# Eight dense column blocks of the first expert table, later choices for the second row block, earlier dot products and two rings of query weights

## The chip, the cores and the metric

The kernel runs on one core of a Trainium2 chip. The time is the device time of one execution in microseconds (us): lower is better. Five engines take part, each with its own queue of instructions: TensorE (PE, with its weight loads listed apart as PEld), VectorE (DVE), ScalarE (ACT), GpSimd (POOL) and SyncE (SP). SP issues most plain DMA transfers, POOL the gathers of single rows by index.

## The reference

One decoder layer on 256 prompt tokens and 32 sample tokens: a joint input projection, RWKV-7 heads and sparse-attention heads, an output projection, a layer norm, an expert mixer (PEER) and a second layer norm. The change concerns the first half of the expert mixer. Cut to it:

```python
def peer_ffn(x, wq, subkeys, u_tab, v_tab):            # x: 256 x 2048; 8 heads, 128 keys
    q = (xt @ wq).reshape(n, P_HEADS, 2, P_DKEY // 2)
    s = einsum('nhcd,hckd->nhck', q, subkeys)
    hv, hix = top_k(s, 16)
    cand   = hv[:, :, 0, :, None] + hv[:, :, 1, None, :]
    cand_e = hix[:, :, 0, :, None] * 128 + hix[:, :, 1, None, :]
    tv, tpos = top_k(cand, 16)
    expert = take_along_axis(cand_e, tpos)              # 8 x 16 experts of 16384 per token
    gate = softmax(tv)
    h = gelu(einsum('cd,chkd->chk', xb, u_tab[expert])) # 128 dot products per token
    return einsum('chk,chkd->cd', gate * h, v_tab[expert])
```

The tables `u_tab` and `v_tab` have 16,384 rows of 2,048 numbers each.

## The kernel before

The 256 prompt tokens are two row blocks of 128 (`t` = 0 and 1), a token to a partition. A dot product of a token with one of its chosen rows of the first table is split by columns:

- The first `UG` = 128 x (16 - `NDB`) = 896 columns are gathered. For each of the 2 x 128 pairs of row block and choice, POOL issues one indirect DMA (L454, `rows<-in_peer_u_g,gi`: 128 rows of 896 numbers into one of `NRW` = 5 buffers named `rows`, called by `fetch`), and DVE multiplies them with the tokens (`x1a`) and sums up in one instruction (`dot`, L1794). The indices lie in `gi`. There are 256 such dots.
- The other `NDB` = 9 blocks of 128 columns are computed densely for all 16,384 rows: for each of 128 steps `i1`, SP loads 128 x 1152 numbers of the transposed table (L1864, `ur<-in_peer_u_t`, `NUR` = 5 buffers), PE does nine matmuls against the transposed tokens `Xfd` (L1867), and ACT copies the 128 x 256 sums to `AW` (L1868). The numbers that were chosen are picked from `AW` later, in the weigh stage, and added to the dots.

Ahead of this dense loop stands the query loop over nine steps `h`. In step `h` SP loads the query weights of head `h` (`query_load`, L1711, 512 KB each, a ring of `WB` = 4 buffers `wraw`), PE projects them, and ACT copies the queries to `QP`. The scores of head `h - 1` follow (`scores`, both row blocks, into a ring of four `TB`), and then its choices (`choose`, both row blocks): on DVE three times the top 16 with their indices (L1363 to L1367), the sums over 54 candidates (L1400), and a comparison of each chosen position with an iota (L1409, 128 x 864, into a `rows` buffer `hit`); POOL multiplies `hit` with the candidates' expert numbers (L1411). One step later `settle` sums `hit` up on DVE (L1417) and copies the 16 expert numbers to `gi` on POOL (L1418). DVE also does four dots of the sample tokens (`sr`, L1556) per step. From `h` = 7 one prompt dot per step is put in (`NDW` = 1).

After the query loop stand the softmax of both row blocks (`gates`), and the dense loop with two dots per step `i1` until 256 are done (`dot`). `table(0)` writes the first row block's indices, gates and sums transposed into `TB` within the loop; `table(1)` comes in the weigh stage. That stage reuses the `rows` buffers for its sample rows (`smp_fetch`), and the loads of the second table (`rows_load`, L1971, `v_`) begin in it. Its first load stands on SP's queue wherever the scheduler puts it.

What order the instructions have on each queue is set by a scheduler, which takes the program's order and its own estimates; `issue_after(x)` makes it place what stands inside behind instruction `x`. Buffers come from named pools with a number of copies (`bufs`); a new use waits until the old one is read.

Of the kernel before, what the change touches and what calls it, by code (L numbers as in the profile page):

```python
# [18 lines left out]
P = 128  # L19
# [3 lines left out]
NPR = 256  # L23
# [126 lines left out]
def hybrid_decode_step(ctx: ExitStack, tc: tile.TileContext, a, outs, dbg=None):  # L150
# [1218 lines left out]
    def scores(t, h, pool, QP, SKT, tag):  # L1369


        pb = bank(tag)
        for c in range(2):
            if t < 2:
                pe.matmul(pb[:, 128 * c:128 * c + 128], QP[:, 2 * h + c, P * t:P * t + P], SKT[:, 2 * h + c, :],
                          start=True, stop=True)
            else:
                for g in range(4):
                    k = 2 * (2 * g + h) + c
                    pe.matmul(pb[32 * g:32 * g + 32, 128 * c:128 * c + 128], QP[:, k, :], SKT[:, k, :],  # L1380
                              start=True, stop=True)
        S = TB[:, (2 * h + t) % 4].rearrange("p (a b) -> p a b", a=2) if t < 2 else pool([P, 2, P], "S")
        sc.copy(S.rearrange("p a b -> p (a b)"), pb[:, :256])
        return S

    def choose(t, h, pool, S, TV):

        nb_ = 2 if t < 2 else 1
        HV, HI, HF = (pool([P, 2, 16], nm, ty, bufs=nb_) for nm, ty in (("HV", F32), ("HI", U32), ("HF", F32)))
        for c in range(2):  # L1390
            top16(S[:, c, :], HV[:, c, :], HI[:, c, :])
        k_ = 2.0 if t == 2 else 1.0
        for c in range(2):
            gp.tensor_scalar(HF[:, c], HI[:, c], k_ if c else k_ * P, 0.0, op0=OP.mult, op1=OP.add)

        CV, CE = (pool([P, NCAND], nm, bufs=nb_) for nm in ("CV", "CE"))
        for dst, src, en in ((CV, HV, ve), (CE, HF, gp)):
            o = 0
            for i0, ni, w in CAND:
                en.tensor_tensor(dst[:, o:o + ni * w].rearrange("p (i j) -> p i j", i=ni),  # L1400
                                 src[:, 0, i0:i0 + ni, None].to_broadcast([P, ni, w]),
                                 src[:, 1, None, :w].to_broadcast([P, ni, w]), OP.add)
                o += ni * w
        TI, TF = (pool([P, 16], nm, ty, bufs=nb_) for nm, ty in (("TI", U32), ("TF", F32)))
        hit = up([P, 1024], "rows", bufs=NRW) if t < 2 else pool([P, 1024], "cw", bufs=NCW)
# [3 lines left out]
        i_ = ve.tensor_tensor(hit, iota[:, None, :NCAND].to_broadcast([P, 16, NCAND]),  # L1409
                              TF[:, :, None].to_broadcast([P, 16, NCAND]), OP.is_equal)  # L1410
        gp.tensor_tensor(hit, hit, CE[:, None, :].to_broadcast([P, 16, NCAND]), OP.mult)  # L1411
# [295 lines left out]
    wring = lambda: kw_([P, 8, P], "wraw", bufs=WB)  # L1707
    def query_load(c, o):

        w = wring()  # L1710
        sy.dma_start(w, w_q[:, 128 * c:128 * c + 128].rearrange("(k p) c -> p k c", p=P)[:, o:o + 8])  # L1711
        return w

    wq_ = {(0, o): query_load(0, o) for o in (0, 8)}

    M_("ln1")
# [50 lines left out]
    up([P, 1024], "rows", bufs=NRW)  # L1767
# [3 lines left out]
    dp, kc, kq = (Pool(nm, "left") for nm in ("dp", "kc", "kq"))  # L1771
    dp([P, NDB, P], "ur", bufs=NUR)
    Xfd = dp([P, NDB, NPR], "Xfd")
    SKT = kq([P, 16, P], "SKT")
    QP = kq([P, 16, NPR], "QP")

    dots = [(t, s_) for t in range(2) for s_ in range(P)]
    got, rows_ = [0, 0], {}

    def fetch(upto):  # L1780

        for i in range(got[0], min(upto, len(dots))):
            t, s_ = dots[i]
            rows_[i] = up([P, 1024], "rows", bufs=NRW)[:, :UG]
            gather(rows_[i], a["peer_u_g"], GI[t][:, s_:s_ + 1])
            got[0] = i + 1

    def dot(n=1, upto=2 * P, keep=False, ahead=NRW):

        for i in range(got[1], min(got[1] + n, upto)):  # L1790
            t, s_ = dots[i]
            fetch(min(i + ahead, upto))
            r_, h_ = rows_.pop(i), HD[t][:, s_:s_ + 1]
            i_ = ve.scalar_tensor_tensor(r_, r_, 1.0, X1a[t], op0=OP.mult, op1=OP.mult, accum_out=h_)  # L1794
# [18 lines left out]
    sy.dma_start(SKT, a["subkeys_t"])  # L1813
    hits = []
    for h in range(9):
        S = []
        for c in (2 * h, 2 * h + 1):
            if c < 16:
                pb = bank("pj")
                for o in range(0, 16, 8):  # L1820
                    w = wq_.pop((c, o), None) or query_load(c, o)
                    for k in range(8):
                        pe.matmul(pb[:, :NPR], w[:, k, :], XT[:, o + k, :], start=(o + k == 0), stop=(o + k == 15))
                last_ = sc.copy(QP[:, c, :], pb[:, :NPR])
            if h and c == 2 * h:
                S = [scores(t, h - 1, kc, QP, SKT, "pb") for t in range(2)]
        if h == 2:
            for t in range(2):
                sy.dma_start(X1a[t], X1D[P * t:P * t + P, :UG])
        if h:  # L1830
            late_, hits = hits, []
            for t in range(2):
                chosen, hit = choose(t, h - 1, kc, S[t], TV[t])
                hits.append(hit)
            with tc.issue_after(chosen.ins):
                for t, hit in enumerate(late_):
# [22 lines left out]
    AW = aw([P, 2, NPR, 64], "AW")

    def dense(i1):

        w = dp([P, NDB, P], "ur", bufs=NUR)
        sy.dma_start(w.rearrange("p k e -> p (k e)"), a["peer_u_t"][P * i1:P * i1 + P, :])  # L1864
        ph = bank("ph")
        for e in range(NDB):
            mm = pe.matmul(ph[:, :NPR], w[:, e, :], Xfd[:, e, :], start=(e == 0), stop=(e == NDB - 1))  # L1867
# [74 lines left out]

    x4p([P, 4, P], "oT", bufs=2)
    ws = x4p([P, 32, 32], "ws")
    fs, sr = bank("fs"), {}

    def smp_fetch(j):

        for q in range(2):
            sr[j, q] = up([P, 1024], "rows", bufs=NRW)  # L1950
            gather(sr[j, q], vh2, ig[q][:, j:j + 1])

    def smp_add(j):
# [16 lines left out]
        raw[k] = (vp if k % 3 else vr)([P, FD], "v_", bufs=2 if k % 3 else 1)  # L1970
        return sy.dma_start(raw[k], vtab[P * k:P * k + P, :FD])  # L1971

    dot(2 * P - got[1])
# [178 lines left out]
```

## Time and profile before

| what | us |
|---|---|
| median of 3 runs (lowest, highest) | 2457.12 (2453.75, 2460.82) |
| the profiled execution | 2451.44 |
| its span, first to last instruction | 2449.7 |
| PE busy | 2254.7 (92%) |
| DVE busy | 1748.2 (71%) |
| POOL busy | 1332.6 (54%) |
| ACT busy | 819.9 (33%) |
| all DMA: 684.09 MB | mean 279 GB/s |
| mean granted TensorE clock | 0.950 |

The span lies 1.7 us under the time of the execution. The busy times are totals over stages of different kinds: the input projection and the heads up to about 1040 us, the query loop from about 1050 to 1220, the dense loop from about 1185 to 1696, then the weigh stage and the product with the second table. The change touches the query and the dense loop, so these stretches are read apart.

### The profile page before, as it was taken

Reading aid. Unit: us, or ns where it says so; the run is one execution under the profiler, and the core shown is the slowest. Engines: PE = TensorE matmul, PEld = TensorE weight load, DVE = VectorE, ACT = ScalarE, POOL = GpSimd, SP = SyncE. Lnnn points to the kernel's source line nnn. Section 1 sums busy time; section 2 is a strip of 40 time slices with the busy share of each in tenths; the row PEclk is TensorE's granted clock in tenths of the full one; section 3 lists DMA queues with packets and bytes.
Section 4 is the critical chain, followed back from the end, with each engine's and each line's share of the span. In section 5 each row is a group of like instructions: output and inputs, shape, how many; then the busy total and the mean of one; then the engine's idle time right before and its main releaser. Section 6 shows DMA issues by size and latency. Waiting matters only on the chain.

```text
span 2449.7 us, 42718 instructions
## 1 busy us (share of the span) xinstructions
PE 2254.7 (92%) x15628; PEld 1886.4 (77%) x15628; DVE 1748.2 (71%) x3985; ACT 819.9 (33%) x1591; POOL 1332.6 (54%) x1419
## 2 busy tenths in 40 slices
PE   7989999997988997779989999998998999999996
PEld 7977898884645665568878888887777888887885
DVE  5789766555653456789955555556777799998888
ACT  4433223223431333220111111111777544444343
POOL 5678423233445003567757555666442688876762
PEclk9999999998996996999999999999999999999998
DMA  7887975448668984988499999998664799999994
GB/s 221 233 247 224 281 213 167 136 141 261 213 228 250 312 277 160 320 287 271 147 402 399 400 403 388 390 400 313 190 190 131 280 359 365 357 369 361 353 346 187
DMA packets 327602, 684.09 MB, mean 279 GB/s; under 512 B 82270, under 2 KB 200992, under 8 KB 326464
## 3 DMA queue, kind: packets, MB, share of 16 engines
q1 hardware_dynamic: 246176, 342.58, 42.1%
q0 software_dynamic: 81216, 338.78, 38.4%
q8 instruction: 123, 2.02, 0.3%
q14 instruction: 87, 0.71, 0.1%
HBM read 665.69 MB, written 23.88 MB: 281 GB/s over the span
## 4 chain that ended last, share of the span: by engine, by line
PE 51%; issue 13%; DVE 12%; POOL 11%; DMA 9%; ACT 2%; SPq 1%; POOLq 0%; DVEq 0%; ACTq 0%
PE pb L2066 20%; POOL rows L454 9%; PE pj L423 8%; PE pa L1660 3%; PE px L1904 3%; PE pa L1937 2%; DVE sr L1556 2%; PE p L1080 2%; PE pt L1896 2%; DMA co<-in_cache_cmp_kv,gidx 2%; PE ss L1497 1%; DMA rows<-in_peer_u_g,gi 1%; PE fs L1955 1%; DVE CA L477 1%; DMA co<-in_cache_sel_kv,sidx 1%
## 5 line engine op out<-in xcount | busy, mean ns | idle before, releaser
L1867 PE MATMUL ph<-Xfd,ur 128*128 128x256 f32 x2304 | 500.8, 380 | 10.1 <-DMA ur<-in_peer_u_t 9.7
L1867 PEld LDWEIGHTS ph<-Xfd,ur 128*128 128x128 f32 x2304 | 439.2, 191 | 71.0 <-issue 10.0
L454 POOL DMA_INDIRECT rq<-in_peer_v_g,gi x256 | 377.6, 1475 | 153.2 <-DVE fP L2039 88.4
L1794 DVE SCALAR_TENSOR_TENSOR rows<-rows,x1a 128x896 f32<-128x896 f32 x256 | 282.0, 1103 | 197.0 <-DMA rows<-in_peer_u_g,gi 195.9
L454 POOL DMA_INDIRECT rows<-in_peer_u_g,gi x256 | 293.1, 1145 | 184.8 <-DVE rows L1794 152.8
L423 PE MATMUL pj<-XH,wl 128*128 128x288 f32 (+1 forms) x752 | 232.2, 309 | 11.3 <-DVE wl L418 6.4
L423 PE MATMUL pj<-XH,wh 128*128 128x288 f32 (+1 forms) x752 | 230.4, 306 | 13.0 <-DVE ss L753 5.9
L2039 DVE SCALAR_TENSOR_TENSOR fP<-rq,ge,fP 128x640 f32<-128x640 f32 x254 | 223.7, 881 | 7.8 <-DMA rq<-in_peer_v_g,gi 5.5
L423 PE MATMUL pj<-XL,wh 128*128 128x288 f32 (+1 forms) x752 | 226.6, 301 | 0.0
L1868 ACT COPY AW<-ph 128x256 f32<-128x256 f32 x128 | 77.0, 609 | 405.9 <-PE ph L1867 400.2
L2066 PE MATMUL pb<-vl,ah 128*128 128x512 f32 (+1 forms) x768 | 207.0, 378 | 0.8
L2066 PE MATMUL pb<-vh,al 128*128 128x512 f32 (+1 forms) x768 | 205.3, 375 | 0.0
L2066 PE MATMUL pb<-vh,ah 128*128 128x512 f32 (+1 forms) x768 | 186.7, 378 | 13.4 <-ACT vh L2058 10.9
L416 ACT CAST wh<-wraw 128x512 fp32r<-128x512 f32 (+1 forms) x188 | 114.6, 616 | 224.1 <-PE pj L423 178.5
L2066 PEld LDWEIGHTS pb<-vh,ah 128*128 128x128 f32 x768 | 144.8, 195 | 35.7 <-ACT vh L2058 13.9
L477 DVE SCALAR_TENSOR_TENSOR CA<-co,wbc,CA 128x256 f32<-128x256 f32 x248 | 135.9, 586 | 49.7 <-DMA co<-in_cache_cmp_kv,gidx 49.7
L2066 PEld LDWEIGHTS pb<-vl,ah 128*128 128x128 f32 x768 | 144.9, 195 | 23.0 <-DVE vl L2059 3.8
L423 PEld LDWEIGHTS pj<-XH,wl 128*128 128x128 f32 (+1 forms) x752 | 144.4, 192 | 22.4 <-DVE wl L418 9.1
L2066 PEld LDWEIGHTS pb<-vh,al 128*128 128x128 f32 x768 | 145.0, 194 | 19.4
L423 PEld LDWEIGHTS pj<-XH,wh 128*128 128x128 f32 (+1 forms) x752 | 144.9, 193 | 19.4 <-DVE ss L753 6.4
L423 PEld LDWEIGHTS pj<-XL,wh 128*128 128x128 f32 (+1 forms) x752 | 144.9, 193 | 1.5 <-issue 1.2
L418 DVE TENSOR_TENSOR wl<-wraw,wh 128x512 fp32r<-128x512 f32 (+1 forms) x141 | 100.2, 720 | 40.0 <-ACT wh L416 39.8
(844 smaller groups left out, 4331.4 us busy)
## 6 DMA issues: line engine op xcount, KB each, us to landing
ur<-in_peer_u_t SPq DMA_DIRECT2D x128, 576.0 KB
wraw<-in_w_in SPq DMA_DIRECT2D x152, 256.0 KB
cw<-in_w_out SPq DMA_DIRECT2D x32, 512.0 KB
wraw<-in_w_out SPq DMA_DIRECT2D x32, 512.0 KB
wraw<-in_peer_wq SPq DMA_DIRECT2D x32, 512.0 KB
cw<-in_peer_wq SPq DMA_DIRECT2D x32, 512.0 KB
wraw<-in_w_in SPq DMA_DIRECT2D x64, 128.0 KB
co<-in_state_win_kv SPq DMA_DIRECT2D x16, 512.0 KB
```

Source lines behind the costliest of these rows:

```text
L416: sc.copy(wh[:, :, :n], w[:, :, :n])
L418: i_ = en.tensor_tensor(wl[:, :, :n], w[:, :, :n], wh[:, :, :n].bitcast(F32), OP.subtract)
L423: last[2] = pe.matmul(pb[:n, :nt], wi[:, k, :n], xi[(o + k) // 8][:, (o + k) % 8, :nt], start=(o + k == 0 and wi is wh and xi is xh), stop ...
L454: gp.indirect_dma_start(out=dst, out_offset=None, in_=rows_, in_offset=bass.IndirectOffsetOnAxis(ap=ix, axis=0))
L477: ve.scalar_tensor_tensor(d_, x_, w_, d_, op0=OP.mult, op1=OP.add)
L1660: pe.matmul(acc[t], xi[:, e, P * t:P * t + P], wi[:, e, :], start=(k == e == n_ == 0), stop=(k == 6 and e == 1 and n_ == 2))
L1794: i_ = ve.scalar_tensor_tensor(r_, r_, 1.0, X1a[t], op0=OP.mult, op1=OP.mult, accum_out=h_)
L1867: mm = pe.matmul(ph[:, :NPR], w[:, e, :], Xfd[:, e, :], start=(e == 0), stop=(e == NDB - 1))
L1868: return mm, sc.copy(AW[:, i1 // 64, :, i1 % 64], ph[:, :NPR])
L1904: pin(pe.matmul(px[:, 128 * e:128 * e + 128].rearrange("p (c j) -> p c j", c=2), oT[:, e, :], AW[:, :, 4 * u + e, :], start=True, stop=True))
L2039: ve.scalar_tensor_tensor(fP[t], r_, w_, fP[t], op0=OP.mult, op1=OP.add)
L2066: pe.matmul(acc[3 * t + q][:, :n_], wi[:, P * t:P * t + P], xi[:, 512 * q:512 * q + n_], start=(k == 0 and wi is ah and xi is vh), stop=(k ...
```

## The change

- `NDB` goes from 9 to 8: a block load has 1,024 columns, PE does eight matmuls per step, and a gathered row has 1,024 numbers (`UG` = 1024).
- The query loop does the choices of the first row block only. The second row block's scores are kept in `S1`; its choices are done in the dense loop by a new generator, `choose_parts`, whose six parts per head are spread, with the dots, over the first 80 steps (`NCB` = 10 steps per head). There DVE does all of it, ACT copies the expert numbers, and it has buffers of its own but for `hit`, which is one of the five `rows`. `gates(1)` follows at step 80, `table(0)` at step 90.
- From `h` = 3 on, `NDW` = 5 dots are put into each query step: 30 in all. The other 226 are spread evenly over the 128 dense steps.
- Query weights go through two rings: the first half of each column group through a second ring `wraw2` of 4 buffers, the other half through `wraw`. `QP` becomes a ring of six.
- The two loads of `x1a` are placed behind the 13th and behind the last query weight, and all loads of `ur` behind the last query weight.
- The `rows` buffers get a pool of their own that ends with the dense loop; the weigh stage takes other ones.

```diff
-NDW = 1
-ND = 1
-NDN = 8
+NDW = 5
+NCB = 10
-NDB = 9
+NDB = 8
...
-        S = TB[:, (2 * h + t) % 4].rearrange("p (a b) -> p a b", a=2) if t < 2 else pool([P, 2, P], "S")
+        S = (TB[:, h % 4], S1[:, h])[t].rearrange("p (a b) -> p a b", a=2) if t < 2 else pool([P, 2, P], "S")
...
+    def choose_parts(h, pool, S, TV):
+        HV, HI, HF = (pool([P, 2, 16], nm, ty) for nm, ty in (("HVb", F32), ("HIb", U32), ("HFb", F32)))
+        for c in range(2):
+            top16(S[:, c, :], HV[:, c, :], HI[:, c, :])
+            yield 1
...
+        TI, TF = (pool([P, 16], nm, ty) for nm, ty in (("TIb", U32), ("TFb", F32)))
+        top16(CV, TV[:, h, :], TI)
+        ve.tensor_copy(TF, TI)
+        yield 1
+        hit = rp([P, UG], "rows", bufs=NRW)[:, :16 * NCAND].rearrange("p (a b) -> p a b", a=16)
+        ve.tensor_tensor(hit, iota[:, None, :NCAND].to_broadcast([P, 16, NCAND]),
+                         TF[:, :, None].to_broadcast([P, 16, NCAND]), OP.is_equal)
+        ve.tensor_tensor(hit, hit, CE[:, None, :].to_broadcast([P, 16, NCAND]), OP.mult)
+        yield 1
+        EF = pool([P, 16], "EFb")
+        ve.tensor_reduce(EF, hit, AX.X, OP.add)
+        sc.copy(GI[1][:, 16 * h:16 * h + 16], EF)
+        yield 1
...
-        w = wring()
-        sy.dma_start(w, w_q[:, 128 * c:128 * c + 128].rearrange("(k p) c -> p k c", p=P)[:, o:o + 8])
+        w = wring() if c == 0 or o else kq([P, 8, P], "wraw2", bufs=4)
+        wl_.append(sy.dma_start(w, w_q[:, 128 * c:128 * c + 128].rearrange("(k p) c -> p k c", p=P)[:, o:o + 8]).ins)
...
-        if h == 2:
-            for t in range(2):
+        if h in (3, 8):
+            with tc.issue_after(wl_[12 if h < 8 else -1]):
+                t = h // 8
                 sy.dma_start(X1a[t], X1D[P * t:P * t + P, :UG])
...
-            for t in range(2):
-                chosen, hit = choose(t, h - 1, kc, S[t], TV[t])
-                hits.append(hit)
+            chosen, hit = choose(0, h - 1, kc, S[0], TV[0])
+            hits.append(hit)
             with tc.issue_after(chosen.ins):
...
-                if h > 6:
+                if h > 2:
                     dot(NDW, 16 * (h - 1), ahead=2)
...
+        with tc.issue_after(wl_[-1]):
+            sy.dma_start(w.rearrange("p k e -> p (k e)"), a["peer_u_t"][P * i1:P * i1 + P, :])
...
+    later, early = seq(*(choose_parts(h, kc, S1[:, h].rearrange("p (a b) -> p a b", a=2), TV[1]) for h in range(8))), got[1]
     for i1 in range(P):
         mm, end = dense(i1)
-        n_ = ND + (i1 * NDN % 8 < NDN)
-        dot(min(max(P - got[1], 0) or n_, n_))
-        if got[1] == P + 24:
+        n_ = early + -(-(2 * P - early) * (i1 + 1) // P)
+        dot(n_ - got[1])
+        with tc.issue_after(last_dot[0].ins):
+            for _ in take(later, 6 * (i1 + 1) // NCB - 6 * i1 // NCB):
+                pass
+            if i1 == 8 * NCB:
+                for _ in later:
+                    pass
+                gates(1, up, TV[1])
+        if i1 == 8 * NCB + 10:
```

Where the instructions stand. First SP's queue from the first query weights on; `wraw` are query weights, `SKT` the sub-keys, `x1a` the tokens' first columns (the later ones of 512 are parameters of the last layer norm), `ur` blocks of the first table, `v_` rows of the second. Before:

```order
L1711 DMA wraw<-in_peer_wq 128x8x128
L1813 DMA SKT<-in_subkeys_t 128x2048
L1711 DMA wraw<-in_peer_wq 128x8x128 x5
L1829 DMA x1a<-x1d 128x896 x2
L1711 DMA wraw<-in_peer_wq 128x8x128
L1864 DMA ur<-in_peer_u_t 128x1152 x5
L1711 DMA wraw<-in_peer_wq 128x8x128 x21
L1864 DMA ur<-in_peer_u_t 128x1152 x5
L1971 DMA v__17742<-in_peer_v 128x1408
L1864 DMA ur<-in_peer_u_t 128x1152 x70
```

The same queue now, from the last query weights to the first blocks, and at its end (numbers behind a name tell the buffers of the second ring apart). First:

```order
L1741 DMA wraw_12951<-in_peer_wq 128x8x128
L1741 DMA wraw<-in_peer_wq 128x8x128
L1862 DMA x1a<-x1d 128x1024
L1896 DMA ur<-in_peer_u_t 128x1024 x86
L2045 DMA x1a<-in_ln_g 32x512
```

All query weights now stand ahead of the first block. At the end of the blocks:

```order
L2045 DMA x1a<-in_ln_b 32x512
L2045 DMA x1a<-in_ln_g 32x512
L2045 DMA x1a<-in_ln_b 32x512
L1896 DMA ur<-in_peer_u_t 128x1024 x41
L2013 DMA v__17636<-in_peer_v 128x1408
L2043 DMA x1a<-x1d 32x512 x4
```

The load of the second table moved from behind the tenth block to behind the last.

Next DVE in the middle of the query loop, from one head's last top 16 to the next head's scores (`TV` holds the chosen scores, `TI` and `TF` their positions, `CT` the iota, `EF` the expert numbers). Before:

```order
L1366 MAX TV_12152<-CV 128x8
L1366 MAX TV_12153<-CV 128x8
L1367 MAX_INDEX TI<-TV_12152,CV 128x8
L1367 MAX_INDEX TI<-TV_12153,CV 128x8
L1408 CAST TF<-TI 128x16 x2
L1409 TENSOR_TENSOR rows<-CT_61,TF 128x864 x2
L1417 TENSOR_REDUCE EF<-rows 128x16 x2
L1556 SCALAR_TENSOR_TENSOR sr,shT<-sr,sx_12077 128x1024 x4
L1363 MAX HV<-TB 128x8 x4
L1364 MAX_INDEX HI<-HV,TB 128x8 x2
```

DVE at such a place now:

```order
L1407 CAST TF<-TI 128x16
L1408 TENSOR_TENSOR rows<-CT_61,TF 128x864
L1447 TENSOR_REDUCE EF<-rows 128x16
L1586 SCALAR_TENSOR_TENSOR sr,shT<-sr,sx_12077 128x1024 x4
L1825 SCALAR_TENSOR_TENSOR rows,hd_12150<-rows,x1a 128x1024 x2
L1362 MAX HV<-TB 128x8 x2
L1363 MAX_INDEX HI<-HV,TB 128x8 x2
L1399 TENSOR_TENSOR CV<-HV 128x8
L1399 TENSOR_TENSOR CV<-HV 128x10
L1825 SCALAR_TENSOR_TENSOR rows,hd_12150<-rows,x1a 128x1024
L1364 MATCH_REPLACE TB<-HV,TB 128x128
L1399 TENSOR_TENSOR CV<-HV 128x12
```

Every instruction of the choices stands once where it stood twice, and dots (L1825) stand before and between them.

Last DVE in the dense loop. Before, from the last indices that `table` turns (L1805, L1806) to the first picks of the weigh stage (`oo`); `hd_12150` and `hd_12151` take the sums of the first and of the second row block:

```order
L1806 CAST ii<-ii 128x128
L1805 TENSOR_SCALAR ii<-gi_71 128x128 x2
L1794 SCALAR_TENSOR_TENSOR rows,hd_12150<-rows,x1a 128x896
L1806 CAST ii<-ii 128x128 x3
L1794 SCALAR_TENSOR_TENSOR rows,hd_12150<-rows,x1a 128x896 x124
L1794 SCALAR_TENSOR_TENSOR rows,hd_12151<-rows,x1a 128x896 x128
L1892 TENSOR_TENSOR oo<-CT_61,TB 128x1024 x2
```

There the dense loop holds dots alone. Now the parts of the second row block's choices stand between the dots, here for the end of one head:

```order
L1432 CAST TFb<-TIb 128x16
L1825 SCALAR_TENSOR_TENSOR rows,hd_12150<-rows,x1a 128x1024 x3
L1435 TENSOR_TENSOR rows<-CT_61,TFb 128x864
L1437 TENSOR_TENSOR rows<-rows,CEb 128x864
L1825 SCALAR_TENSOR_TENSOR rows,hd_12150<-rows,x1a 128x1024 x2
L1440 TENSOR_REDUCE EFb<-rows 128x16
L1825 SCALAR_TENSOR_TENSOR rows,hd_12150<-rows,x1a 128x1024 x3
L1362 MAX HVb<-S_12169 128x8
```

Two dots stand between the product that fills the `hit` buffer and the sum that frees it.

More of the change, by code (lines that the diff above doesn't have):

```diff
@@ L1386, in choose @@
     def choose(t, h, pool, S, TV):
-        nb_ = 2 if t < 2 else 1
+        nb_ = 1
         HV, HI, HF = (pool([P, 2, 16], nm, ty, bufs=nb_) for nm, ty in (("HV", F32), ("HI", U32), ("HF", F32)))
@@ L1404, in choose @@
         TI, TF = (pool([P, 16], nm, ty, bufs=nb_) for nm, ty in (("TI", U32), ("TF", F32)))
-        hit = up([P, 1024], "rows", bufs=NRW) if t < 2 else pool([P, 1024], "cw", bufs=NCW)
+        hit = rp([P, UG], "rows", bufs=NRW) if t < 2 else pool([P, 1024], "cw", bufs=NCW)
         hit = hit[:, :16 * NCAND].rearrange("p (a b) -> p a b", a=16)
@@ L1412, in choose @@
         return i_, hit
+    def choose_parts(h, pool, S, TV):
[3 more added lines that the diff above has]
+            yield 1
+        for c in range(2):
+            ve.tensor_scalar(HF[:, c], HI[:, c], 1.0 if c else 1.0 * P, 0.0, op0=OP.mult, op1=OP.add)
+        CV, CE = (pool([P, NCAND], nm) for nm in ("CVb", "CEb"))
+        for dst, src in ((CV, HV), (CE, HF)):
+            o = 0
+            for i0, ni, w in CAND:
+                ve.tensor_tensor(dst[:, o:o + ni * w].rearrange("p (i j) -> p i j", i=ni),
+                                 src[:, 0, i0:i0 + ni, None].to_broadcast([P, ni, w]),
+                                 src[:, 1, None, :w].to_broadcast([P, ni, w]), OP.add)
+                o += ni * w
+        yield 1
[11 more added lines that the diff above has]
+        sc.copy(GI[1][:, 16 * h:16 * h + 16], EF)
+        yield 1
     def settle(t, h, pool, hit):
@@ L1766, in hybrid_decode_step @@
     TV = [up([P, 8, 16], f"TV{t}") for t in range(2)]
-    up([P, 1024], "rows", bufs=NRW)
     xa_ = up([P, 2 * UG], "x1a")
@@ L1770, in hybrid_decode_step @@
     TB = up([P, 4, NPR], "TB")
-    dp, kc, kq = (Pool(nm, "left") for nm in ("dp", "kc", "kq"))
+    rp, dp, kc, kq = (Pool(nm, "left") for nm in ("rp", "dp", "kc", "kq"))
+    rp([P, UG], "rows", bufs=NRW)
+    S1 = dp([P, 8, 2 * P], "S1")
     dp([P, NDB, P], "ur", bufs=NUR)
@@ L1783, in fetch @@
             t, s_ = dots[i]
-            rows_[i] = up([P, 1024], "rows", bufs=NRW)[:, :UG]
+            rows_[i] = rp([P, UG], "rows", bufs=NRW)
             gather(rows_[i], a["peer_u_g"], GI[t][:, s_:s_ + 1])
@@ L1796, in dot @@
                 tc.keep_in_program_order(i_)
-            got[1] = i + 1
+            got[1], last_dot[:] = i + 1, [i_]
     def table(t):
@@ L1815, in hybrid_decode_step @@
     for h in range(9):
-        S = []
+        S, QP = [], {2 * h - 2 + c: q_ for c, q_ in enumerate(QN)} if h else {}
+        QN = [kq([P, NPR], "QP", bufs=6) for c in range(2)]
         for c in (2 * h, 2 * h + 1):
@@ L1849, in hybrid_decode_step @@
     kw_.close()
-    for q in range(0, NDB, 3):
-        sc.copy(Xfd[:, q:q + 3, :], XT[:, 16 - NDB + q:19 - NDB + q, :])
+    for q in range(0, NDB, 4):
+        sc.copy(Xfd[:, q:q + 4, :], XT[:, 16 - NDB + q:20 - NDB + q, :])
     xq.close()
@@ L1855, in hybrid_decode_step @@
     banks(ph=5, pb=3)
-    for t in range(2):
-        gates(t, up, TV[t])
+    gates(0, up, TV[0])
     aw = Pool("aw", "right")
@@ L1878, in hybrid_decode_step @@
     dp.close()
+    rp.close()
     x4p, vr = Pool("x4", "left"), Pool("vr", "right")
@@ L1944, in hybrid_decode_step @@
     ws = x4p([P, 32, 32], "ws")
+    x4p([P, 1024], "rows", bufs=NRW)
     fs, sr = bank("fs"), {}
@@ L1949, in smp_fetch @@
         for q in range(2):
-            sr[j, q] = up([P, 1024], "rows", bufs=NRW)
+            sr[j, q] = x4p([P, 1024], "rows", bufs=NRW)
             gather(sr[j, q], vh2, ig[q][:, j:j + 1])
@@ L1971, in rows_load @@
         return sy.dma_start(raw[k], vtab[P * k:P * k + P, :FD])
-    dot(2 * P - got[1])
     at = lambda j: 2 + 55 * j // 31
```

11 lines of the change are left out of this document (5 added, 6 removed).

## The prediction

> **What bounds the kernel now.** I read the page first, then busy time by stage, then the DMA answer, the waits and the timeline of the two stages that the change touches. The page's first line and its three largest groups here:
>
> ```profile
> PE 2254.7 (92%) x15628; PEld 1886.4 (77%) x15628; DVE 1748.2 (71%) x3985; ACT 819.9 (33%) x1591; POOL 1332.6 (54%) x1419
> ...
> L1867 PE MATMUL ph<-Xfd,ur 128*128 128x256 f32 x2304 | 500.8, 380 | 10.1 <-DMA ur<-in_peer_u_t 9.7
> ...
> L1794 DVE SCALAR_TENSOR_TENSOR rows<-rows,x1a 128x896 f32<-128x896 f32 x256 | 282.0, 1103 | 197.0 <-DMA rows<-in_peer_u_g,gi 195.9
> L454 POOL DMA_INDIRECT rows<-in_peer_u_g,gi x256 | 293.1, 1145 | 184.8 <-DVE rows L1794 152.8
> ```
>
> PE looks like the bound (92%). The stages say more. Each row below is a stretch: start and end, length, busy us (instructions) of PE, PEld, DVE, ACT and POOL, then granted clock, DMA share and GB/s.
>
> ```profile
> 1050.00:1110.00 60.00, 48.49 (x213) 41.23 (x212) 50.21 (x145) 12.73 (x34) 43.57 (x51) 0.91 1.01 334
> 1110.00:1185.00 75.00, 74.98 (x369) 66.45 (x368) 75.00 (x310) 7.61 (x22) 58.58 (x97) 1.00 0.78 240
> 1185.00:1240.00 55.00, 44.87 (x196) 38.43 (x195) 46.92 (x178) 7.82 (x16) 34.94 (x56) 0.91 0.57 201
> 1240.00:1690.00 450.00, 450.00 (x2089) 396.09 (x2088) 263.68 (x480) 71.05 (x117) 274.88 (x239) 1.00 1.01 396
> 1690.00:1701.00 11.00, 6.77 (x32) 5.49 (x30) 7.46 (x15) 1.39 (x3) 8.87 (x8) 0.97 0.84 273
> ```
>
> In the 450 us of the dense stage PE never stops, and the DMA engines are just as full: share 1.01 at 396 GB/s. Before it, the share is 0.78 for 75 us and 0.57 for 55 us: 16.5 + 23.7 = 40.2 us in which the DMA engines had nothing to do, while DVE was full (75.00 of 75).
>
> ```profile
> GB/s 409 407 410 405 380 409 407 381 400 410 407 408 408 399 376 406 409 385 404 409 406 383 356 375 410 405 379 383 404 372 409 408 383 391 405 408 408 390 391 341
> DMA packets 35908, 178.13 MB, mean 396 GB/s; under 512 B 5745, under 2 KB 5745, under 8 KB 35878
> ...
> q0 software_dynamic: 19150, 109.77, 62.1%
> q1 hardware_dynamic: 16728, 67.98, 38.5%
> ```
>
> That is the DMA answer for 1240 to 1690: q0 carries the gathers (3,584 B rows), q1 the blocks of the transposed table (4,608 B rows). Both cost 0.57% of the engines per MB, so bytes set the price, not rows. The waits of 1235 to 1690, as total us, times and longest:
>
> ```profile
> DVE rows L1794 <- DMA rows<-in_peer_u_g,gi: 188.7, 234, 2.5
> POOL rows L454 <- DVE rows L1794: 148.9, 159, 2.6
> ```
>
> DVE waits for rows, and POOL waits for DVE to free one of the five row buffers: the gathers turn as fast as the DMA engines let them. So two bounds end together, PE at 1695.96 and the last dot at 1700.2:
>
> ```profile
> 1184.86 27.36 PE L1867 MATMUL ph<-Xfd,ur 128*128 128x256 f32 x126
> ...
> 1234.27 25.92 PE L1867 MATMUL ph<-Xfd,ur 128*128 128x256 f32 x107 [9.66 <-DMA ur<-in_peer_u_t]
> ...
> 1497.23 198.73 PE L1867 MATMUL ph<-Xfd,ur 128*128 128x256 f32 x920
> ```
> ```profile
> 1699.10 1.11 DVE L1794 SCALAR_TENSOR_TENSOR rows<-rows,x1a 128x896 f32<-128x896 f32 x1
> ...
> 1700.14 2.35 DVE L1892 TENSOR_TENSOR oo<-CT,TB 128x1024 f32<-128x1024 f32 x2
> ```
>
> **The change, part by part.** The sum is made on the profiled execution (2451.44 us, span 2449.7), which lies 5.7 us under the median of the runs, 2457.12; I subtract the difference from the median.
>
> *Eight blocks for nine, on PE.* The trace counts each of these matmuls twice (2304 = 128 x 9 x 2). 920 in 198.73 us is 0.216 us each; 256 fewer make 55.3 us less, 442.4 us for 2048. Begun at about 1185, PE would be done near 1628. This is not the gain, because the second bound stays.
>
> *Eight blocks for nine, in bytes.* Traffic of 1040 to 1701, with KB of each issue, or median us to landing for the gathers:
>
> ```profile
> DMA packets 74088, 230.26 MB, mean 348 GB/s; under 512 B 7297, under 2 KB 35969, under 8 KB 73916
> ...
> ur<-in_peer_u_t SPq DMA_DIRECT2D x128, 576.0 KB
> ...
> rows<-in_peer_u_g,gi POOLq DMA_INDIRECT x256, 7.6
> ```
>
> A block shrinks by 64 KiB (128 x 65,536 B = 8.4 MB less), a gather grows by 64 KiB (256 x 65,536 B = 16.8 MB more), one 0.7 MB load of the second table leaves this stretch, and the x rows grow by 0.1 MB. Net +7.8 MB. At 396 GB/s that is **+19.7 us** for whoever is bound by DMA.
>
> *28 more dots before the dense stage.* They move 28 x 0.524 = 14.7 MB, 37 us of DMA time, ahead of 1240, where 40.2 us stand empty. DVE must carry them, and it was full. A head of the old loop, both row blocks, from its first MAX8 to the next head's:
>
> ```profile
> 1104.21 0.86 DVE L1363 MAX8 HV<-TB 128x8 f32<-128x128 f32 x4
> ...
> 1111.54 2.02 DVE L1409 TENSOR_TENSOR rows<-CT,TF 128x864 f32<-128x864 f32 x2
> 1113.48 2.01 DVE L1417 TENSOR_REDUCE EF<-rows 128x16 f32<-128x864 f32 x2
> 1115.40 2.81 DVE L1556 SCALAR_TENSOR_TENSOR sr<-sr,sx 128x1024 f32<-128x1024 f32 x1
> ...
> 1118.14 1.21 DVE L1556 SCALAR_TENSOR_TENSOR sr<-sr,sx 128x1024 f32<-128x1024 f32 x1
> ...
> 1119.29 1.21 DVE L1556 SCALAR_TENSOR_TENSOR sr<-sr,sx 128x1024 f32<-128x1024 f32 x1
> ...
> 1121.58 0.86 DVE L1363 MAX8 HV<-TB 128x8 f32<-128x128 f32 x4
> ```
>
> A head takes 17.4 us; the choices of two row blocks 11.2, so 5.6 for one. Taking one out and five dots in (1,024 wide as these sr rows, 1.15 us from start to start, so 5.75) leaves 17.5 us. DVE stays at its old pace and finishes the first row block's choices near 1220 as before, but with some 25 to 30 dots done instead of 6. POOL gets lighter: 8 of its 16 products go to DVE.
>
> ```profile
> L1411 POOL TENSOR_TENSOR rows<-rows,CE 128x864 f32<-128x864 f32 x16 | 36.5, 2301 | 10.3 <-DVE rows L1409 10.3
> ```
>
> How much of the 40.2 us is filled? All of it (0 left) if a transfer always waits in line; 24 left if only 12 of the 28 land early, since in the new order a dot stands behind the choices that free its buffer. The order puts 14 dots ahead of the seventh head's product and the rest among heads 7 and 8, where the share was lowest, and the stretch asks for more than the engines have. I take 6 left: **-34.2 us**.
>
> *Two rings, and the SP queue.* The old queue stands behind one load of the second table while PE runs dry (the 9.66 us above):
>
> ```profile
> SPq L1971 <- POOL gi L1418: 19.1, 1, 19.1
> ```
>
> In the new order this load stands behind all blocks, so the wait goes, and its 0.7 MB arrive in the 200 us of the weigh stage. Five blocks no longer stand ahead of query weights; they come behind the last one. PE then has 57 us in hand over the stage's end; what late weights or blocks cost it, up to that, costs nothing. I price all of it at zero; if PE became the bound again, each us would count.
>
> *Second row block's choices among the blocks, on DVE.* 8 x (5.6 + 1.05 for the product at L1409's rate + 5 small sums and 2 scalings of 0.15 to 0.2) is about 62 us, up to 77 if nothing overlaps without a twin. With 226 dots of 1.15 us it makes 322 to 337 us in some 480: DVE is not the bound, and its 188.7 us of waiting absorb it. But the hit tile takes one of the five row buffers for one or two dots. A gather on four buffers needs (7.6 landing + 1.15)/4 = 2.2 us; the pace that DMA allows is 0.524 MB/(396 - 151 for the blocks) = 2.14 us. Almost no loss; bounds 0 and 25 us (each head's is_equal, product and reduction, 3.1 us, laid bare). Nearest is the row of DVE's wait (0.8 us a dot, more than is added per dot). I take **+3**.
>
> *The tail.* PE done at 1628, some 40 gathers run alone. They need 1.32 us of DMA each; POOL issued them 1.3 us apart when nothing held it, and the shortest landing is 4.3 us:
>
> ```profile
> 1221.47 0.95 POOL L454 DMA_INDIRECT rows<-in_peer_u_g,gi x1 [0.31 <-DVE sm L1427]
> 1222.79 0.97 POOL L454 DMA_INDIRECT rows<-in_peer_u_g,gi x1 [0.16 <-POOL gi L1418]
> ```
> ```profile
> DMA to landing us min/median/max: 4.3/7.6/11.1
> ```
>
> So 1.32 to 1.45 us each: 0 to 6 us, I take **+2**. Here a page bears on who is served first. The Trainium skill, "DMA: Bandwidth & Descriptors", section on queues, rings and completion order, says that each DMA engine takes turns between the queues that have work, packet by packet. By that, blocks get up to half of 396, above the 151 that PE asks, so PE runs ahead and leaves the tail to gathers (2448); if gathers pushed blocks back instead, both would end together and the 2 us would go (2446).
>
> Sum: +19.7 - 34.2 + 3 + 2 = -9.5 us. 2457.1 - 9.5 = **2447.6 us**. What comes before 1040 and after the last dot keeps its order.
>
> **The rivals.**
> *DMA has room above 396 (faster).* The better slices of the GB/s row reach 405 to 410. For: PE was as full as DMA, so gathers may only have kept pace with PE. Against: DVE's wait for rows in 234 of 243 dots. At 410 the last 450 us shrink by 3.4%, 15 us: 2432. The Trainium skill, "DMA: Bandwidth & Descriptors", section on where 436 GB/s comes from, puts the ports' ceiling at 435; no run here shows it, and by it the stretch would lose about 40 us.
>
> *It cancels (no change).* With 15.5 us left empty instead of 6, the sum is 0: 2457. For: 40.2 us is a mean over a loop with bursts. Against: the stretch's demand.
>
> *DVE stalls in order (slower).* A dot stands between two choices and its gather takes 7.6, under load 11.1 us; each such wait delays the choices behind it, hence the indices, hence the free run of gathers. It decides from 15.5 us left empty; at 3 us for each of 8 heads, 24 us more stay empty (30 in all), and the sum is +14.5: 2472.
>
> *The hit tile starves the gathers (slower).* The 25 us bound in place of 3: 2470.
>
> That the dots don't come early is excluded by the order.
>
> **How the numbers follow.** Runs of this kernel lie within 0.15% of their median, so I call 0.3% (7.4 us) the least that can be told. Forecast 0.45 (its own range 2438 to 2454; four fifths of it beyond 0.3%), room above 396 0.13, cancels 0.22 (0.17 within), stalls 0.14, hit tile 0.06. Faster: 0.40 + 0.13 + 0.03 = 0.56. Slower: 0.13 + 0.05 + 0.02 = 0.20. Same: 0.24. The range takes in the room above 396 and most of the stalls: 2432 to 2468.
>
> **What would show it.** Right: share above 0.9 from 1110 to 1240; PE done with the blocks near 1630, the last dot near 1690; gathers about 2.1 us apart while PE runs and under 1.5 after; no wait of SP for POOL; DVE's wait for rows still the longest. Wrong: share under 0.85 before 1240, DVE waiting several us per head in the query stage, gathers over 2.3 us apart among the choices, or PE still busy at the last dot.

## The result and the profile after

The changed kernel takes 2477.11 us (median of 8 runs; before 2457.09, also 8): a ratio of 1.0103, interval 1.0068 to 1.0138. It is 1% slower; the prediction was 2447.6 us, in 2432 to 2468. The profiled execution has a span of 2476.4 us, 26.7 more than before: the last dot ends at 1723.7 instead of 1700.2 (+23.5), and what follows takes 752.7 instead of 749.5.

The page's totals and two groups, and then POOL's gathers in the view of groups by line with all that ended their idle time:

```profile
PE 2193.8 (89%) x15372; PEld 1831.9 (74%) x15372; DVE 1803.8 (73%) x4049; ACT 822.7 (33%) x1600; POOL 1326.2 (54%) x1347
...
L1899 PE MATMUL ph<-Xfd,ur 128*128 128x256 f32 x2048 | 442.4, 379 | 0.0
...
L1825 DVE SCALAR_TENSOR_TENSOR rows<-rows,x1a 128x1024 f32<-128x1024 f32 x256 | 313.2, 1229 | 124.9 <-DMA rows<-in_peer_u_g,gi 123.4
```
```profile
L453 POOL DMA_INDIRECT rows<-in_peer_u_g,gi x256 | 305.0, 1191 | 237.7 <-DVE rows L1825 121.6 <-issue 47.2 <-DVE ii L1837 28.2
```

PE's blocks take 442.4 us without a pause, as forecast. What has grown is the last item of POOL's row: 28.2 us behind DVE's `ii`, where it was 0.4. By stretch (columns as in the prediction's table):

```profile
1110.00:1185.00 75.00, 74.93 (x371) 66.45 (x370) 63.69 (x213) 8.10 (x22) 59.86 (x67) 1.00 1.05 356
1185.00:1240.00 55.00, 55.00 (x257) 48.41 (x256) 41.67 (x92) 10.62 (x19) 39.03 (x39) 1.00 0.86 310
...
1540.00:1560.00 20.00, 20.00 (x94) 17.62 (x93) 6.90 (x11) 3.64 (x6) 5.64 (x5) 1.00 0.89 338
1560.00:1580.00 20.00, 20.00 (x94) 17.60 (x94) 2.91 (x9) 3.11 (x7) 1.14 (x1) 1.00 0.48 157
...
1660.00:1680.00 20.00, 0.00 (x0) 0.00 (x0) 13.80 (x25) 0.00 (x0) 16.31 (x13) 0.50 0.90 312
```

The early stage went as forecast: the DMA share is 1.05 and 0.86 where it was 0.78 and 0.57, and DVE is no longer full. Then two things go wrong. From 1548 to 1577 DVE and POOL nearly stop (2.91 and 1.14 us of 20) while PE works on: a hole. And PE is done at 1624.7 (no busy time in the last row), after which gathers run alone for 99 us: POOL issues 13 in 20 us, at 312 GB/s.

The hole in DVE's timeline, then in ACT's (start, length, in brackets the wait ahead and for whom):

```profile
1547.25 1.05 DVE L1440 TENSOR_REDUCE EFb<-rows 128x16 f32<-128x864 f32 x1
1577.09 0.36 DVE L1836 TENSOR_SCALAR ii<-gi 128x128 int32<-128x128 int32 x2 [28.79 <-ACT gi L1441]
```
```profile
1548.81 0.60 ACT L1900 COPY AW<-ph 128x256 f32<-128x256 f32 x1 [2.83 <-PE ph L1899]
...
1576.44 0.60 ACT L1900 COPY AW<-ph 128x256 f32<-128x256 f32 x1 [2.86 <-PE ph L1899]
1576.83 0.22 ACT L1441 CAST gi<-EFb 128x16 int32<-128x16 f32 x1
```

DVE's sum of the eighth head is done at 1548.3. Its copy into `gi` is a 0.22 us instruction on ACT, but on ACT's queue it stands behind copies of dense sums (nine rows from 1548.81 to 1576.44), each of which waits for PE, 3.45 us a block. DVE, whose next instruction reads `gi`, stands 28.79 us, and the dots behind it with it. That instruction is no dot: it is the first of `table(1)`, which the scheduler has put there. By then 172 of the 256 dots were done, so the next ones were of the second row block's third head, whose numbers had long been written. What held them was the order on DVE's queue, not a number that they needed.

In the tail the waits of DVE and POOL, 1630 to 1722, then four of POOL's issues and three of DVE's dots:

```profile
DVE rows L1825 <- DMA rows<-in_peer_u_g,gi: 23.7, 32, 2.6
POOL rows L453 <- issue: 13.4, 44, 0.3
POOL rows L453 <- DVE rows L1825: 8.0, 9, 2.1
```
```profile
1683.04 1.68 POOL L453 DMA_INDIRECT rows<-in_peer_u_g,gi  x1 [0.63 <-DVE rows L1825]
1685.03 0.95 POOL L453 DMA_INDIRECT rows<-in_peer_u_g,gi  x1 [0.30 <-issue]
1686.28 0.94 POOL L453 DMA_INDIRECT rows<-in_peer_u_g,gi  x1 [0.30 <-issue]
1687.95 1.82 POOL L453 DMA_INDIRECT rows<-in_peer_u_g,gi  x1 [0.73 <-DVE rows L1825]
```
```profile
1682.69 1.22 DVE L1825 SCALAR_TENSOR_TENSOR rows<-rows,x1a 128x1024 f32<-128x1024 f32 x1
...
1686.45 1.23 DVE L1825 SCALAR_TENSOR_TENSOR rows<-rows,x1a 128x1024 f32<-128x1024 f32 x1 [1.30 <-DMA rows<-in_peer_u_g,gi]
...
1687.72 1.23 DVE L1825 SCALAR_TENSOR_TENSOR rows<-rows,x1a 128x1024 f32<-128x1024 f32 x1
```

POOL waits for a buffer in 9 of 53 gathers; for the rest it goes from one issue to the next (0.30 us between). An issue takes 0.95 us, but the two here that begin while a dot runs take 1.68 and 1.82: both end 0.81 to 0.82 us after the dot does (1683.91 and 1688.95), as if they had to wait for it. Overlap alone does not do it: the issue at 1686.28, in which a dot begins 0.17 us later, takes 0.94. All 256 issues of this trace say the same. 97 began with a dot under way that had over 0.14 us to run; they took 1.62 us in the median, and 87 of them ended 0.80 to 0.84 us after that dot. In 107 others a dot began only later; 102 of these took 1.00 us or less.

### The profile page after: what moved, and what is told of

It is laid out like the page before. It is cut to its first block, busy times and chain, and to the rows that moved or that the text cites. A ratio compares the mean times of both kernels' runs of the same rounds, so it can differ in the third digit from the quotient of the medians.

```text
span 2476.4 us, 42041 instructions
## 1 busy us (share of the span) xinstructions
PE 2193.8 (89%) x15372; PEld 1831.9 (74%) x15372; DVE 1803.8 (73%) x4049; ACT 822.7 (33%) x1600; POOL 1326.2 (54%) x1347
## 4 chain that ended last, share of the span: by engine, by line
PE 69%; DMA 10%; DVE 8%; issue 6%; POOL 5%; ACT 2%; SPq 1%; DVEq 0%; POOLq 0%; ACTq 0%
PE pb L2107 19%; PE ph L1899 16%; PE pj L422 7%; PE pj L1855 4%; PE px L1945 3%; PE pa L1978 2%; PE pa L1690 2%; PE p L1079 2%; POOL rows L453 2%; PE pt L1937 2%; DMA rows<-in_peer_u_g,gi 1%; PE ss L1527 1%; DMA big<-in_state_rwkv 1%; PE fs L1997 1%; DMA co<-in_cache_cmp_kv,gidx 1%
## 5 line engine op out<-in xcount | busy, mean ns | idle before, releaser
L1899 PE MATMUL ph<-Xfd,ur 128*128 128x256 f32 x2048 | 442.4, 379 | 0.0
L453 POOL DMA_INDIRECT rows<-in_peer_u_g,gi x256 | 305.0, 1191 | 237.7 <-DVE rows L1825 121.6
L1899 PEld LDWEIGHTS ph<-Xfd,ur 128*128 128x128 f32 x2048 | 389.0, 190 | 52.8
L1825 DVE SCALAR_TENSOR_TENSOR rows<-rows,x1a 128x1024 f32<-128x1024 f32 x256 | 313.2, 1229 | 124.9 <-DMA rows<-in_peer_u_g,gi 123.4
```

The costliest lines, as they stand in the source:

```text
L453: gp.indirect_dma_start(out=dst, out_offset=None, in_=rows_, in_offset=bass.IndirectOffsetOnAxis(ap=ix, axis=0))
```

## The experiments

Times are told as ratios to the kernel before on the same chip. The profiled executions enter the dense loop between 4 us earlier and 23 us later than that of the changed kernel, so traces are compared from PE's first block to the last dot: before 515.3 us, changed 541.6.

**The copy alone to DVE.**

```diff
-        sc.copy(GI[1][:, 16 * h:16 * h + 16], EF)
+        ve.tensor_copy(GI[1][:, 16 * h:16 * h + 16], EF)
```

> The copy of the second row block's expert numbers is done by DVE instead of ACT; nothing else is changed. Theory A (DVE stands 28.8 us behind a copy that sits on ACT's queue behind ACT's copies of the dense sums, and the gathers stand with it): the 28.8 us wait is gone, about 13 more gathers are done while PE runs, the gather-only tail after PE shrinks from 57 gathers to about 44, and the time falls by about 22 us, to 2455. Rival B (the wait is harmless, since DMA bandwidth sets the end and is caught up later): the last dot moves by under 5 us, time 2472 to 2477.

Ratio 1.0109 (1.0041 to 1.0176): nothing won. But the wait was not gone; the waits of 1240 to 1840 have it under another name:

```profile
DVE sm L1456 <- ACT ge L1455: 38.1, 1, 38.1
```

The second softmax takes its exponential on ACT (`ge`), behind the same copies. 56 gathers were left when PE was done, as many as in the changed kernel. So this run tells nothing of the price of the wait, only that the link was not the one instruction.

**No wait for ACT.** The copy on DVE, and the softmax behind the last dot:

```diff
             if i1 == 8 * NCB:
                 for _ in later:
                     pass
-                gates(1, up, TV[1])
...
+    with tc.issue_after(last_dot[0].ins), tc.issue_after(end.ins):
+        gates(1, up, TV[1])
```

> As changed, but DVE waits for nothing of ACT in the dense loop: DVE copies the second row block's expert numbers itself, and the second softmax (its exponential runs on ACT) stands behind the last dot instead of at step 80. Theory A (the wait for ACT holds DVE and the gathers some 29 to 38 us, whichever instruction carries it; with only the copy moved it went on to the softmax): no wait of DVE for ACT over 3 us, about 43 gathers left when PE is done instead of 56, and 22 us less than the changed kernel: 0.1% above the kernel before (ratio 1.001). Rival B (the DMA engines make up for the hole): ratio 1.010 as before.

Ratio 1.0010 (0.9982 to 1.0038), as theory A had it. DVE's only long wait for ACT in the dense loop is gone, 40 gathers are left when PE is done instead of 56, and first block to last dot takes 515.2 us, 26.4 less. Both move 192.5 MB in that time, at 355 GB/s as changed and at 374 here. The wait for ACT is shown as the cause of the loss against before; without it the change is worth nothing either way. Whether it would do to leave the copy on ACT, and to move only `table(1)` and the softmax behind the last dot, was not run.

**What sets the pace of the tail.** The same kernel with shorter dots:

```diff
-            i_ = ve.scalar_tensor_tensor(r_, r_, 1.0, X1a[t], ...)
+            i_ = ve.scalar_tensor_tensor(r_[:, :256], r_[:, :256], 1.0, X1a[t][:, :256], ...)
```

> As the one without waits for ACT, but each dot multiplies only the first 256 of its 1,024 gathered columns (the other products are left out); the gathers are the same. It asks what sets the 1.7 us per gather in the tail. Theory P (POOL's issue, which takes 0.95 us alone and up to 1.99 us while DVE works): POOL's mean falls from 1.28 to about 1.0 us and a gather to 1.3 us. Theory Q (five buffers, each busy for landing, dot and hand-over): 1.5 us. Theory R (the DMA engines themselves are nearly full with gathers alone: share 0.91 at 316 GB/s): 1.5 to 1.6 us at a share of 1.

POOL's gathers of the tail by line and a stretch of the tail, first of the kernel without waits for ACT, then of this one (a single execution, 2431.9 us):

```profile
L453 POOL DMA_INDIRECT rows<-in_peer_u_g,gi x39 | 51.0, 1309 | 16.1 <-issue 9.8 <-DVE rows L1825 6.4
```
```profile
1645.00:1700.00 55.00, 0.00 (x0) 0.00 (x0) 40.78 (x67) 0.00 (x0) 43.14 (x34) 0.50 0.88 308
```
```profile
L454 POOL DMA_INDIRECT rows<-in_peer_u_g,gi x26 | 24.6, 946 | 11.4 <-DVE rows L1826 9.6 <-issue 1.8
```
```profile
1640.00:1670.00 30.00, 0.00 (x0) 0.00 (x0) 9.44 (x43) 0.00 (x0) 20.55 (x22) 0.50 1.02 405
```

With DVE busy for a third of the time instead of three quarters, POOL's issue falls from 1309 to 946 ns, a gather from 1.66 us, issue to issue in these stretches, to 1.40, and gathers alone move 405 GB/s, at a share of 1.02. P's signs came, nearly to the size (1.3 forecast), and R is refuted: the engines were not nearly full before. The 1.40 also lies under the 1.5 that Q forecast for five buffers. What counts is how issue and dot meet, not DVE's load as such: in the version with seven row buffers below, the last six gathers go 1.26 us apart beside full dots, with issues of 0.95 to 0.97 us, since there each dot begins some 0.2 us after an issue. The Trainium skill, "SBUF — State Buffer", section on the two separate sides, says that DVE and GpSimd share a pair of ports as an exclusive lock: a DVE operation with two SBUF inputs and a GpSimd operation that reads SBUF shut each other out, and whichever starts first has the pair for its whole instruction. The dot has two such inputs and a gather reads its indices from `gi`; the 87 issues that end 0.8 us behind a dot agree with it. The other direction is not seen: the dot that began 0.17 us into an issue took its usual 1.23 us.

**Fewer early dots**, with the waits for ACT still there:

```diff
-NDW = 5
+NDW = 1
...
-                if h > 2:
+                if h > 6:
```

> As changed, but with 2 dots ahead of the dense loop as before instead of 30. If 28 early dots really ran in idle DMA time, they come back as 28 more gathers of the tail: 28 x 1.7 us = 48 us, time about 2525. By the prediction's own price (37 us of DMA time at 396 GB/s, 3 of it lost) it is about 2511. If the early dots won nothing: 2477.

Ratio 1.0209 (1.0125 to 1.0293), 26 us above the changed kernel by the ratios, but with some 22 us either way; 24.8 by the traces, first block to last dot. 71 gathers are left when PE is done instead of 56: of 28 early dots at most 15 count. The other 13 are made good while PE runs, since the DMA engines had room in 1185 to 1240 (share 0.73 without them): by 1240 this run has done 16 dots, the changed kernel 31. A hole that is 7.5 us longer (36.3) clouds the sum. So the early dots are worth some 17 to 25 us by the traces, less than both forecasts, 48 and 34; the times alone exclude neither.

**Nine blocks** with the rest of the change, with and without the waits for ACT:

```diff
-NDB = 8
+NDB = 9
```

> Nine blocks and 896 gathered columns as in the kernel before, with the rest of the change kept (early dots, two rings, choices in the dense loop, the copy on ACT). Theory C (eight blocks move work from PE, which keeps 128 columns at no DMA loss, to the gathers, which alone don't fill the DMA engines): PE again works to about 1684, the gathers end at about the same time, even with the wait for ACT, there is no tail, and the time is about 2443, faster than before. Rival D (the early dots and the choices among the blocks cost time themselves): 2457 or more.

> Nine blocks, and DVE waits for nothing of ACT. Theory C (with nine blocks PE sets the end, without a pause from the first block to the last): the same as nine blocks with the waits, ratio 0.990 to 0.996, PE 497 us for its blocks and the last dot within 5 us of PE's end or before it. Rival G (the gathers still set the end there): 10 us or more less than that, ratio under 0.989.

Ratios 0.9935 (0.9904 to 0.9965) and 0.9943 (0.9916 to 0.9971): faster than before, and the waits make no difference; but there DVE's only long wait for ACT was 7.3 us (for `ge`), not 28.8, so this is no test of the full wait. PE in the run with the waits, and the stretch in which both ends fall:

```profile
L1899 PE MATMUL ph<-Xfd,ur 128*128 128x256 f32 x2304 | 497.6, 379 | 0.0
```
```profile
1680.00:1720.00 40.00, 35.94 (x170) 29.34 (x168) 28.21 (x70) 9.55 (x18) 20.00 (x16) 0.83 0.77 266
```

PE works 497.6 us without a pause, and no gather is left when it ends. What C forecast of time and tail came in both runs, and D and G fell. C's reason is shown in part only. The tail of gathers alone is slow (313 GB/s from 1633.9 to 1706.5 with eight blocks and no wait for ACT), but from the first block to the last dot that kernel moves 192.56 MB at 374 GB/s, and the one with nine blocks 183.80 MB at 367. So the 0.7% that the ninth block saves against eight (1.0010) is borne by the bytes that nine blocks need not move, not by a better rate. The kernel before moves 192.00 MB at 373 GB/s in that stretch; with nine blocks and the rest of the change it is less, since 16 gathers are issued ahead of PE's first block.

**Row and block buffers.** The two kinds of buffer are 4 KiB a partition each, so one can be paid for with the other: ten in all, as in the changed kernel. Seven and three, first with the waits for ACT, then without:

```diff
-NUR = 5
+NUR = 3
-NRW = 5
+NRW = 7
```

> Seven row buffers instead of five, paid for with three block buffers instead of five; the wait for ACT stays. It asks what sets 1.7 us per gather in the tail after PE is done. Theory P (POOL's issue: 1.28 us of instruction and 0.30 us between two): the tail stays at 1.58 us or more per gather, time about 2468. Rival Q (five buffers: landing 6.0, dot 1.2 and hand-over, about 8 us over five): the tail falls to about 1.35 us per gather, time about 2455. If three block buffers starve PE, its end moves beyond 1630 and the tail is shorter for that reason.

> As the one without waits for ACT, with seven row and three block buffers: the pair that came out at a ratio of 1.030 with ACT's waits in it. Theory L (it was slow because ACT's copies for PE stood behind copies that waited for DVE, and so held PE): without that link PE ends within 15 us of the last dot, ratio 0.985 to 0.995. Rival M (three block buffers starve PE by themselves): PE ends 30 us or more after the last dot, ratio over 1.00.

Ratios 1.0296 (1.0231 to 1.0361) and 1.0303 (1.0266 to 1.0340): far slower, and ACT was not the reason, nor did the first of the two answer its question, since no gather-only tail was left: the last dot came at 1664, PE's last block at 1793. Theory L fell. The waits of PE and of SP in the run without ACT's waits:

```profile
PE ph L1899 <- DMA ur<-in_peer_u_t: 130.9, 14, 68.6
```
```profile
SPq L2046 <- DVE S L1364: 64.3, 1, 64.3
SPq L2044 <- DVE ii L1836: 53.8, 1, 53.8
```

L2046 and L2044 load parameters of the last layer norm and the sample rows into the space of `x1a`, once the dots no longer read it: they go out at 1420.0 and 1649.8, as the 128th and the last dot end. The scheduler had put them behind the 48th and 94th block on SP's queue, so that all later blocks waited for dots. Taking them out of the blocks' way, for seven and three, and for six and four:

```diff
-            sy.dma_start(w.rearrange("p k e -> p (k e)"), a["peer_u_t"][P * i1:P * i1 + P, :])
+            ul_[:] = [sy.dma_start(w.rearrange("p k e -> p (k e)"), a["peer_u_t"][P * i1:P * i1 + P, :])]
...
         if s_ == 24:
+            with tc.issue_after(ul_[0].ins):
...
```

> As seven row and three block buffers without waits for ACT, and the loads of the last layer norm's parameters and of the sample rows into x1a stand behind the last block on SP's queue instead of in the midst of the blocks. Theory O (those loads wait for dots of DVE, 64.3 and 53.8 us, and hold the blocks behind them and so PE): no pause of PE over 10 us, PE's end within 15 us of the last dot, ratio 0.985 to 0.995. Rival M (three block buffers starve PE by themselves): PE ends 30 us or more after the last dot, ratio over 1.00.

> As the one without waits for ACT, with six row buffers and four block buffers instead of five and five. Theory E (the buffers in flight set how the two streams share the DMA engines, and it is the gathers alone at the end that lose): the blocks get less, PE ends later, near 1690 us where the last dot is too, the gather-only tail is under 20 gathers, ratio about 0.994. Rival F: four block buffers starve PE beyond that, PE ends last, over 1710 us, and the ratio is over 1.00.

> The same for six row and four block buffers. Theory O: SP's wait of 18.4 us and PE's pause of 16.7 us go, PE is done about 443 us after its first block, the tail has some 8 gathers more and grows by 8 x 1.7 us less the 16.7 us: time the same within 4 us, ratio 0.989 to 0.993. Rival S (the pause was what brought the two streams together, and the sixth buffer alone does little): ratio 0.996 or more.

Seven and three turns from 1.0303 to 0.9880 (0.9845 to 0.9915): a third queue in order was the cause (theory O), not three block buffers. These do slow PE somewhat, to 472 us for its blocks instead of 443, but with no pause over 3 us, and PE is done 14.5 us before the last dot. Six and four gave 0.9907 (0.9872 to 0.9941) with the loads in the way and 0.9913 (0.9885 to 0.9941) without, so its 16.7 us pause of PE did no harm, as theory O expected, and S fell. Theory E had the gathers left right (19, under 20) but not the reason: PE was done at 1639.5, not near 1690; F fell.

**Which of the two buffers did it.** Four block buffers and five row buffers; and the same with a buffer of its own for `hit`:

```diff
-NUR = 5
+NUR = 4
...
-        hit = rp([P, UG], "rows", bufs=NRW)[:, :16 * NCAND]...
+        hit = rp([P, 16 * NCAND], "hitb", bufs=1)[:, :16 * NCAND]...
```

> As the one without waits for ACT, with four block buffers instead of five, five row buffers. Theory J (four block buffers give the gathers more of the DMA engines, since PE now waits at times): PE ends 10 us or more later than 443 us after its first block, the tail has 35 gathers or fewer, ratio about 0.996. Rival K (PE never waits for blocks with four either; the sixth row buffer made the gain): PE 442 us, 40 gathers in the tail, ratio 1.001.

> As the one without waits for ACT, with four block buffers, and the hit tile of the choices in a buffer of its own, so that all five row buffers serve gathers. Theory H (the hit tile's share of the five row buffers is what held the gathers to 2.20 us each while PE ran): 2.1 us, some 8 gathers fewer in the tail, ratio about 0.995. Rival I (the six row buffers won by more packets in flight all the time, not by the hit tile): ratio as with five row buffers, 1.001.

Ratios 0.9992 (0.9967 to 1.0016) and 0.9999 (0.9973 to 1.0026), with 38 and 35 gathers left. Neither fewer block buffers nor the hit tile's place explains the gain: the ratios of K and I came. J and H were wrong by the ratio, though PE did take 450.8 us instead of K's 442, and with the hit tile apart the trace shows 400 GB/s beside 394 from 1240 to 1630, a gain too small for these ratios. The sixth row buffer explains it: six and four against five and four, both with the loads in the way, is 0.9907 against 0.9992. The DMA traffic of the dense stretch with five, six and seven row buffers (1240 to 1630, the last to 1655, in GB/s also by fortieths for the first and the last), of the kernel without waits for ACT, then of the two with the loads out of the way:

```profile
GB/s 411 408 410 408 373 396 410 402 339 394 410 408 388 397 404 410 353 404 411 408 381 409 409 410 331 400 410 410 377 407 403 405 370 411 410 409 406 408 405 339
DMA packets 42621, 154.57 MB, mean 396 GB/s; under 512 B 4818, under 2 KB 4818, under 8 KB 42595
```
```profile
DMA packets 43478, 157.67 MB, mean 404 GB/s; under 512 B 4917, under 2 KB 4917, under 8 KB 43452
```
```profile
GB/s 409 409 409 409 409 410 407 409 411 408 410 409 408 409 404 410 410 409 408 409 409 408 409 407 409 409 398 385 402 410 409 406 409 410 408 409 409 408 409 408
DMA packets 46411, 169.22 MB, mean 408 GB/s; under 512 B 5156, under 2 KB 5156, under 8 KB 46385
```

396, 404 and 408 GB/s: the best slices are the same, 410 or 411, but with five buffers the rate falls in every fourth slice, and with seven it hardly does. Eight of the low slices (331 to 388) lie where DVE ends a head's choices, or right behind; at the first of these POOL waits 4.05 us for a row buffer. That more gathers in flight carry the engines over such gaps fits this, but is not shown apart. The 40 gathers left when PE is done become 29 and 7. First block to last dot goes from 515.2 to 491.6 and 486.7 us, for the same 192 to 193 MB. Seven and three, with no wait for ACT and the loads behind the blocks, is the best version here: 2427.34 us beside 2457.99 of before.

## Why the prediction was wrong, point by point

- **Bounds before** (two, ending together) and **PE's part** (done near 1628, 55 us less): right, 1624.7. The spread of 0.15% rested on three runs; later runs of the kernel before lie up to 0.8% from their median.
- **28 early dots** (-34.2 us): the mechanism was right (24 dots done by 1222, where before had 2), and so was the idle share left (14% of 55 us, 7.7; forecast 6), but the size was too large. Taking them away cost 24.8 us by the traces, 7.5 of them for a longer hole, since part of that idle time fills by itself once PE's blocks begin.
- **The choices on DVE** (+3): this is the step that failed. I priced DVE's own work and the hit tile, and put ACT's copy of the indices down as nothing, without asking what stands ahead of it on ACT's queue. There it was tied to PE's pace, and DVE stood 28.8 us. Without the tie the gathers left at PE's end were 40, the number forecast; with it 56. The 16 more cost 26.4 us by the traces, and 0.9% by the ratios. The hit tile, which I weighed instead, changes the time by nothing that the ratios can tell (0.9992 and 0.9999).
- **The tail** (+2; 1.32 to 1.45 us a gather): under-sized. I took the 1.3 us between POOL's issues from two issues that no dot was under way to hold. With DVE at its dots a gather of the tail takes 1.66 to 1.71 us; with short dots it took 1.40. On 40 gathers that is some 10 us (40 x 0.26).
- **Together**: the last dot was forecast at 1690.7 (1700.2 less 9.5) and came at 1723.7, 33 us later: 26.4 of the hole and some 10 of the tail, less the 3.3 by which PE was done earlier. That this closes so well is in part luck: the early dots brought less than forecast, and the bytes took less, and these two errors have opposite signs.
- **Eight blocks for nine in bytes** (+19.7): the ratios of nine and eight without waits for ACT, 0.9943 and 1.0010, make 16 us, with some 10 either way. The term holds, as far as these runs can tell.
- **Two rings and SP's queue**, at zero: PE had no pause, as said. But I looked only at the load that left the block stream, not at the parameter loads that had stayed in it.
- **The rivals**: room above 396 GB/s is real (408), though only with more buffers. "DVE stalls in order" had the right kind of mechanism and a time near the result, in the wrong place: DVE did stall in order, in the dense loop behind ACT, not in the query loop behind gathers. Of the signs that I gave, the run had those for "right" up to 1240 (a share of 0.97 in the mean of 1110 to 1240), and PE's end; it failed on the pace of the tail (under 1.5 us forecast) and on the last dot. Among the choices the gathers came 2.2 us apart, under the 2.3 named as a sign of being wrong. In the chances, four fifths of 0.45 are 0.36, not the 0.40 in the sum; no forecast hangs on it.

## What to carry to other kernels

When an instruction moves to another engine, read what stands ahead of it on that engine's queue and what each of those waits for: a 0.2 us copy behind work paced by a third engine holds whoever needs it by that pace, in either direction, and so does a small load on the queue of a stream. Move the whole link, and look for its twin, before judging the wait's price. Where two streams share the DMA engines, count the buffers in flight of each, and let neither be left alone at the end: here the same work took 0.988 or 1.030 of the time with the same buffers, depending on where a few small loads stood.

## What was not expected of the hardware

- An indirect DMA's issue on POOL took 0.95 us alone, and up to 1.99 us while DVE ran dots of 1,024 columns. What lengthened it was a dot already under way when it began: 87 of 97 such issues ended 0.80 to 0.84 us after that dot. A dot that began later in the issue did nothing to it in 102 of 107 cases.
- A DMA share of 1.01 did not mean that no more could be moved: at shares of 1.01, 1.02 and 1.03, five, six and seven row buffers gave 396, 404 and 408 GB/s.
